# Products of the second block with one 512-column matmul over both parts of the activations, in units of two column tiles

## The chip, the cores and the metric

The kernel runs on one core of a Trainium2 chip. The metric is the device time of one execution in microseconds (us), taken as the median of several runs. Inside the core, TensorE (PE) multiplies matrices and accumulates into PSUM (8 banks of 512 fp32 values on each of 128 partitions); VectorE (DVE), ScalarE (ACT) and GpSimd (POOL) do elementwise work; SyncE (SP) issues the DMAs that bring the weights. "PEld" is TensorE's weight load, which runs beside its matmuls. A "column" of a matmul here is one token of the moving operand.

## The reference

Two blocks in sequence on 256 tokens of 2048 features. The first (a hybrid of a state-space part and a gated delta rule, with modulation) is not touched by the change. The second is two layers of differential attention with a gated short convolution beside it, and an MLP:

```python
def second_block(x, w_in, w_out, conv_w, q_norm_g, k_norm_g, ..., w_up, w_down, rel_bias):
    for l in range(DEPTH_2):                       # 2 layers
        h = _rmsnorm(x, attn_norm_g[l])
        proj = h @ w_in[l]                         # 2048 -> 6 * 1024
        q, k, v, gate_b, gate_c, conv_in = jnp.split(proj, splits, axis=-1)
        ...
        attn = _diff_attention(q, k, v, lam, rel_bias)      # 8 heads
        ...
        conv = gate_b * _short_conv(gate_c * conv_in, conv_w[l])
        x = x + jnp.concatenate([attn, conv], axis=-1) @ w_out[l]     # 2048 -> 2048
        hm = _rmsnorm(x, mlp_norm_g[l]) @ w_up[l]                     # 2048 -> 8192
        x = x + jnp.square(jax.nn.relu(hm)) @ w_down[l]               # 8192 -> 2048
    return x
```

All weights and activations are fp32.

## The kernel before

All big products work on numbers split in two: a high part, rounded to float32r, and a low part, the rest. A product of a weight W and an activation a is summed as hi(W)·hi(a) + hi(W)·lo(a) + lo(W)·hi(a).

Weights arrive in blocks of 512 KB (1024 columns of 128 partitions, `block`, L171). SP issues the load of a block (L177) into one of three `raw` buffers. Each block is split in two halves of 512 columns (`split`): ACT writes the high part (L143), and DVE the low part (L130), except that POOL writes the low parts of every fourth block. The high halves have four buffers and two more, the low halves four.

Activations are kept as pairs [128, 2, 4, 256]: part (high, low), K tile within a group of four, token. `pick` (L438) gives the two parts of one K tile.

`proj_steps` (L191) forms feature-major products: for each K tile of 128 features and each tile of 128 output columns, three matmuls of 256 columns, with the weights as the stationary operand. They all add into one accumulator `acc`, [128, 4, 256], which takes two banks of PSUM; there are two such accumulators (`pa`). A unit is four tiles of columns over all K tiles, 64 triples of matmuls for 16 K tiles, and a block of weights holds two K tiles of it. `proj_tok` (L224) does the values, with the activations as stationary operand and 512 columns of weights as the moving one.

`layer` (L1089) runs: the norm of the input (`norm_in`, L1038), which for the first layer makes its K tiles one after the other on DVE and ACT while the first products already use them; queries and keys (four units); values; then eight attention heads beside the gated convolution. The convolution has six units of eight blocks, 48 steps, and a head starts at each fifth step (`HEADS`, L1324). A head is a chain through the engines: scores on PE, scale and bias on DVE, exponentials on ACT, the difference of the two maps on DVE, transposes on PE (L150), a copy on ACT, the product with the values on PE. After it come `w_out` (four units), the norm, and the MLP, which alternates `up` (two units of 16 K tiles) and `down` (four units of eight K tiles, each added onto `x`). An accumulator is read by one DVE instruction of 1024 columns a unit, for example

```python
                ps = self.proj(wu, 4, act)
                t = self.t4(B)
                self.stt(t, ps, 0.0, rb, ALU.max, ALU.mult)
```

The order on each engine is made when the program is built, by a scheduler that simulates the engines; the generators `convs` and `heads` only give it the order of emission. In the rows below, lines L130, L133, L143, L146 and L150 are the helpers for DVE or POOL two-tensor operations, DVE three-operand ones, ACT, matmul and transpose.

Of the kernel before, what the change touches and what calls it, by code (L numbers as in the profile page):

```python
# [20 lines left out]
D = 2048  # L21
# [10 lines left out]
class Kern:  # L32
# [119 lines left out]
    def rsqrt(self, out, in_, mul, add, x, t):  # L152
        """out = 1/sqrt(in_*mul + add); x and t are scratch of the same shape."""
# [14 lines left out]
    def paced(self, out, in_):  # L168
        """A load that is not due yet, behind the last block of weights."""
# [3 lines left out]
    def block(self, ap, kt):  # L173
        """A block of weights in two parts, by K tile."""
# [16 lines left out]
    def proj_steps(self, w, nt, act, N=T, kts=range(NK), ps=None, fine=False):  # L191
        """Feature-major product: [128, nt, N] of nt tiles of columns over all K tiles, a block of weights a step
        or, if fine, a K tile."""
        ps = self.acc([128, nt, N]) if ps is None else ps
        per_bank = max(1, 512 // N)
        kts = list(kts)
        kt = CW // (nt * 128)
        for k0 in range(0, len(kts), kt):
            hv, lv = self.block(next(w), kt)
            for kk in range(kt):  # L200
# [15 lines left out]
            if not fine:  # L216
                yield ps

# [4 lines left out]

    def proj_tok(self, w, act):  # L224
        """Token-major product: [128, 2, 512] of four tiles of columns."""
        ps = self.acc([128, 2, 512])
        kt = CW // 512
        for k0 in range(0, NK, kt):
            hv, lv = self.block(next(w), kt)
            for kk in range(kt):  # L230
                k = k0 + kk
                (ah, al), = act(k)
# [8 lines left out]
    def sumsq_add(self, ps, src, first, last):  # L241
        """Add the squares of src [128, n, T], summed over features, to ps on every partition."""
# [88 lines left out]
    def ada_gate(self, m0):  # L331
        """Columns of four tiles from tile m0 for the tokens of x alone, as sums of scaled rows."""
# [25 lines left out]
    def side_step(self):  # L358
        """The part of the modulation that the end of the block needs goes along with its last products."""
# [7 lines left out]
    def block1_inputs(self, early, got):  # L367
        """The modulated inputs; early: the banks of projections that advance with them, four K tiles a step."""
# [33 lines left out]
        self.u_full = lambda k: self.pick(self.u[0])(k) + self.pick(self.u[1])(k)  # L402
# [35 lines left out]
    def pick(pairs):  # L438
        """K tile k of activations kept as pairs of parts, [128, 2, 4, T] for four tiles."""
# [1022 lines left out]
```

## Time and profile before

| | us |
|---|---|
| median of 3 runs | 3319.24 |
| lowest, highest | 3317.6, 3322.36 |
| profiled execution, span | 3319.0 |
| median less the span | 0.24 |
| first block (to the first product of the second) | 0 to about 1020 |
| second block, layer 0 | about 1020 to 2172 |
| of it: convolution and heads | 1206 to 1341 |
| of it: MLP | 1434 to 2172 |
| second block, layer 1 | about 2172 to 3314 |
| PE busy in the span | 3188.6 (96%) |
| DVE, ACT, POOL busy | 62%, 49%, 28% |
| granted TensorE clock, mean over the span | 0.988 |

PE is the engine that is nearly always busy. Since the ends of matmuls are modelled and overlap, the time that one really takes is read from the distance between the starts of consecutive ones, not from the durations. The profiled execution's own time is its span and the 0.24 us to the median of the runs.

### The profile page before, as it was taken

How to read it: one execution, taken by the hardware profiler on the slowest of the kernel's cores; microseconds unless marked ns; L12 is line 12 of the kernel's file. 1: busy time of each engine (PE TensorE's matmuls, PEld its weight loads, DVE VectorE, ACT ScalarE, POOL GpSimd, SP SyncE). 2: the span in 40 equal slices, each digit the busy share in tenths (PEclk: the TensorE clock that was granted, in tenths of full speed). 3: DMA queues.
4: the chain of work that ended last, by engine and by line, in shares of the span. 5: the costliest groups of instructions: out<-in, count | busy, mean ns of one | idle time of the engine just before them, and what ended most of it. 6: DMA issues, size and time to landing. Idle time of an engine off the chain costs nothing.

```text
span 3319.0 us, 65150 instructions
## 1 busy us (share of the span) xinstructions
PE 3188.6 (96%) x25258; PEld 3055.3 (92%) x25258; DVE 2072.2 (62%) x3665; ACT 1623.4 (49%) x3116; POOL 935.4 (28%) x739
## 2 busy tenths in 40 slices
PE   7899999998988999999999999999999999999999
PEld 3498888888887899999999999998999999999999
DVE  6878899998747567554444444555675544444444
ACT  6654444444544455454444444444554544444443
POOL 4614433233353222222222222222223222222221
PEclk9999999999999999999999999999999999999999
DMA  8733423334665455555555555555555555555555
GB/s 298 239 107 102 116 88 82 78 101 139 215 231 181 164 174 167 183 179 181 186 181 184 184 182 185 181 186 165 178 166 184 181 183 180 185 184 184 184 179 178
DMA packets 217607, 566.70 MB, mean 171 GB/s; under 512 B 45808, under 2 KB 69856, under 8 KB 217296
## 3 DMA queue, kind: packets, MB, share of 16 engines
q1 hardware_dynamic: 214976, 555.72, 52.0%
q0 software_dynamic: 1456, 4.65, 0.4%
q8 instruction: 198, 3.24, 0.4%
q10 hardware_dynamic: 864, 2.16, 0.2%
q14 instruction: 113, 0.93, 0.1%
HBM read 552.83 MB, written 9.63 MB: 169 GB/s over the span
## 4 chain that ended last, share of the span: by engine, by line
PE 75%; DVE 12%; DMA 5%; issue 2%; ACT 1%; POOL 1%; SPq 0%; DVEq 0%; ACTq 0%; POOLq 0%
PE acc L146 70%; DVE cc L133 2%; DVE lo L130 2%; PE ps L146 2%; PE p_pg L146 1%; PE p_pc L146 1%; DVE A L133 1%; DMA Am<-w_ada 1%; DVE b L130 1%; DMA W<-w_ada 1%; DMA g<-rows 1%; DMA A<-rows 1%; DVE g L133 1%; DMA raw<-w_in 1%; DVE x L133 0%
## 5 line engine op out<-in xcount | busy, mean ns | idle before, releaser
L146 PE MATMUL acc<-t,hi 128*128 128x256 f32 x12160 | 2228.7, 286 | 14.4 <-DVE t L133 6.3
L146 PEld LDWEIGHTS acc<-t,hi 128*128 128x128 f32 x12160 | 1888.6, 193 | 32.2 <-DVE t L133 9.3
L146 PE MATMUL acc<-t,lo 128*128 128x256 f32 x6080 | 1674.4, 286 | 16.5 <-DVE lo L130 15.5
L143 ACT ACTIVATE hi<-raw 128x512 fp32r<-128x512 f32 x1812 | 1092.9, 627 | 1220.6 <-PE acc L146 805.3
L130 DVE TENSOR_TENSOR lo<-raw,hi 128x512 fp32r<-128x512 f32 x1360 | 995.5, 736 | 803.5 <-PE acc L146 734.7
L146 PEld LDWEIGHTS acc<-t,lo 128*128 128x128 f32 x6080 | 1144.1, 193 | 24.0 <-DVE lo L130 20.0
L130 POOL TENSOR_TENSOR lo<-raw,hi 128x512 fp32r<-128x512 f32 x452 | 601.6, 1333 | 1873.3 <-PE acc L146 1440.3
L146 PE MATMUL acc<-c,hi 128*128 128x256 f32 x2560 | 463.9, 283 | 0.0
L146 PEld LDWEIGHTS acc<-c,hi 128*128 128x128 f32 x2560 | 399.4, 192 | 0.0
L146 PE MATMUL acc<-c,lo 128*128 128x256 f32 x1280 | 362.2, 283 | 0.0
L146 PEld LDWEIGHTS acc<-c,lo 128*128 128x128 f32 x1280 | 245.8, 192 | 0.0
L130 DVE TENSOR_TENSOR x<-x,acc 128x1024 f32<-128x1024 f32 x72 | 87.9, 1221 | 156.3 <-PE acc L146 156.3
L133 DVE SCALAR_TENSOR_TENSOR cc<-src,featv,cc 128x248 f32<-128x248 f32 (+2 forms) x224 | 132.7, 619 | 6.1 <-ACT cc L143 6.1
L133 DVE SCALAR_TENSOR_TENSOR t<-acc,t 128x1024 f32<-128x1024 f32 x32 | 39.2, 1225 | 68.2 <-PE acc L146 68.2
L146 PE MATMUL acc<-hi,t 128*128 128x512 f32 x256 | 81.2, 396 | 0.0
L143 ACT ACTIVATE t<-t 128x1024 f32<-128x1024 f32 (+1 forms) x56 | 59.4, 1060 | 26.5 <-DVE t L133 18.0
L130 POOL TENSOR_TENSOR Am<-A,masks 128x512 f32<-128x512 f32 x32 | 45.0, 1419 | 80.0 <-PE p_pg L146 26.8
L130 POOL TENSOR_TENSOR vT<-vT,W 128x512 f32<-128x512 f32 x28 | 41.3, 1474 | 74.8 <-ACT W L143 54.6
L146 PE MATMUL ps<-t,t 128*128 128x128 f32 (+2 forms) x320 | 60.9, 328 | 0.0
L146 PEld LDWEIGHTS acc<-hi,t 128*128 128x128 f32 x256 | 47.8, 188 | 10.5 <-issue 0.8
L146 PE MATMUL p_pg<-U,W 128*128 128x128 f32 (+1 forms) x384 | 47.0, 265 | 9.7 <-DVE W L130 9.5
L130 DVE TENSOR_TENSOR b<-b,b 64x1 f32<-64x1 f32 (+15 forms) x122 | 53.6, 439 | 2.1
(326 smaller groups left out, 2537.5 us busy)
## 6 DMA issues: line engine op xcount, KB each, us to landing
raw<-w_in SPq DMA_DIRECT2D x298, 512.0 KB, 3.7
raw<-w_up SPq DMA_DIRECT2D x256, 512.0 KB, 3.7
raw<-w_down SPq DMA_DIRECT2D x256, 512.0 KB, 3.9
raw<-w_out SPq DMA_DIRECT2D x96, 512.0 KB, 4.1
tok<-w_ada SPq DMA_DIRECT2D x77, 256.0 KB, 4.8
Am<-w_ada SPq DMA_DIRECT2D x57, 256.0 KB, 4.6
W<-w_ada SPq DMA_DIRECT2D x32, 256.0 KB, 4.2
kT<-w_ada SPq DMA_DIRECT2D x26, 256.0 KB, 4.3
```

The costliest lines, as they stand in the source:

```text
L130: return (eng or self.nc.vector).tensor_tensor(out=out, in0=in0, in1=in1, op=op)
L133: (eng or self.nc.vector).scalar_tensor_tensor(out=out, in0=in0, scalar=s, in1=in1, op0=op0, op1=op1)
L143: self.nc.scalar.activation(out=out, in_=in_, func=func, **kw)
L146: return self.nc.tensor.matmul(out, lhsT, rhs, start=start, stop=stop, skip_group_check=skip)
```

## The change

`product` replaces the three matmuls. For an accumulator with a fourth dimension, [128, 2, 2, 256] (tile, part, token), it does two: the high weights over both parts of the activations at once, 512 columns that fill a whole bank, read as two stretches of 256 columns that lie 1024 elements apart in the pair; and the low weights over the high part, 256 columns, onto the second half of the bank. The two halves are added when the accumulator is read: `sum2` copies one half on ACT and adds the other on DVE, `add2` adds both halves onto `x` with two DVE instructions. An accumulator still takes two banks, so that a unit is now two tiles of columns and a block of weights holds four K tiles of it. Queries, keys, convolutions, `w_out`, `up` and `down` use it; the values and the first block keep their matmuls. The weights are laid out on the host in the new order; the bytes loaded are the same. Comments and docstrings are taken out.

```diff
     def proj_steps(self, w, nt, act, N=T, kts=range(NK), ps=None, fine=False):
...
-        per_bank = max(1, 512 // N)
+        per_bank = 1 if isinstance(ps, list) or len(ps.shape) == 4 else max(1, 512 // N)
...
                     o = ps[n][:, 0] if isinstance(ps, list) else ps[:, n]
-                    outs = [o[:, s * T:s * T + T] for s in range(len(sides))]
-                    for s, (o, (ah, al)) in enumerate(zip(outs, sides)):
-                        st = i == 0 and s == 0 and n % per_bank == 0
-                        self.mm(o, hv[kk][:, c], ah, start=st, stop=False, skip=True)
-                        self.mm(o, hv[kk][:, c], al, start=False, stop=False, skip=True)
-                    for o, (ah, al) in zip(outs, sides):
-                        self.mm(o, lv[kk][:, c], ah, start=False, stop=last, skip=True)
+                    self.product(o, hv[kk][:, c], lv[kk][:, c], sides, i == 0 and n % per_bank == 0, last)
...
+    def product(self, o, hw, lw, sides, first, last):
+        if len(o.shape) == 3:
+            self.mm(o.rearrange("p a t -> p (a t)"), hw, sides, start=first, stop=False, skip=True)
+            self.mm(o[:, 1, :], lw, sides[:, 0, :], start=False, stop=last, skip=True)
+            return
...
+    def two_steps(self, w, act, kts=range(NK)):
+        return self.proj_steps(w, 2, act, kts=kts, ps=self.acc([128, 2, 2, T]))
...
+    def sum2(self, out, ps):
+        self.act(out, ps[:, :, 0, :])
+        self.tt(out, out, ps[:, :, 1, :], ALU.add)
+
+    def add2(self, x, ps):
+        for i in range(2):
+            self.tt(x, x, ps[:, :, i, :], ALU.add)
...
-        return lambda k: [(pairs[k // 4][:, 0, k % 4, :], pairs[k // 4][:, 1, k % 4, :])]
+        return lambda k: pairs[k // 4][:, :, k % 4, :]
...
         for u in range(4):
-            ps = self.proj(w, 4, act)
             t = self.t4(B)
-            self.tt(t, ps, rb)
+            for i in range(2):
+                self.sum2(t[:, 2 * i:2 * i + 2], self.two(w, act))
+            self.tt(t, t, rb)
...
         def convs():
-            for g in range(2):
-                for ps in self.proj_steps(w, 4, act):
+            for g in range(4):
...
+                for ps in self.two_steps(w, act):
                     yield
-                gc = self.t4(B)
-                self.tt(gc, ps, rb)
-                self.tt(gc, gc, rb)
+                self.sum2(gc, ps)
+                self.tt(gc, gc, r2)
+                self.tt(gc, gc, r2)
...
         for j in range(4):
-            ps = self.proj(w, 4, cact)
-            self.tt(self.x[j], self.x[j], ps, ALU.add)
+            for i in range(2):
+                self.add2(self.x[j][:, 2 * i:2 * i + 2], self.two(w, cact))
...
             for u in range(2):
-                ps = self.proj(wu, 4, act)
                 t = self.t4(B)
-                self.stt(t, ps, 0.0, rb, ALU.max, ALU.mult)
+                for i in range(2):
+                    self.sum2(t[:, 2 * i:2 * i + 2], self.two(wu, act))
+                self.stt(t, t, 0.0, rb, ALU.max, ALU.mult)
...
             for j in range(4):
-                ps = self.proj(wd, 4, hact, kts=range(8))
-                self.tt(self.x[j], self.x[j], ps, ALU.add)
+                for i in range(2):
+                    self.add2(self.x[j][:, 2 * i:2 * i + 2], self.two(wd, hact, kts=range(8)))
```

On PE at the start of the second block, before (`t_1808` holds the first four K tiles of the norm's output, `t_1809` the next four, `ps` the norm's sum of squares, `acc_12319` the first unit):

```order
L146 MATMUL acc_12319<-t_1808_12194,lo_1_12361 128x256
L146 MATMUL acc_12319<-t_1808_12194,hi_1_12360 128x256 x2
L146 MATMUL acc_12319<-t_1808_12194,lo_1_12361 128x256
L146 MATMUL acc_12319<-t_1809_12211,hi_0_12390 128x256
L146 MATMUL ps_12193<-t_1814_12266,consts 128x256
L146 MATMUL acc_12319<-t_1809_12211,hi_0_12390 128x256
L146 MATMUL acc_12319<-t_1809_12211,lo_0_12391 128x256
```

and the same place after the change, with a second unit, `acc_12427`:

```order
L146 MATMUL acc_12320<-t_1808_12194,hi_1_12327 128x512
L146 MATMUL acc_12320<-t_1808_12194,lo_1_12328 128x256
L146 MATMUL acc_12427<-t_1808_12194,hi_0_12430 128x512
L146 MATMUL acc_12320<-t_1808_12194,hi_1_12327 128x512
L146 MATMUL acc_12320<-t_1808_12194,lo_1_12328 128x256
L146 MATMUL acc_12320<-t_1808_12194,hi_1_12327 128x512
L146 MATMUL acc_12320<-t_1808_12194,lo_1_12328 128x256
L146 MATMUL ps_12193<-t_1814_12266,consts 128x256
L146 MATMUL acc_12320<-t_1809_12211,hi_0_12349 128x512
```

Each K tile now gives two products of the first unit instead of four, and products of the second unit stand among them. Ahead of the first product with K tile 15 stand 60 products before and 44 after.

On PE in the second half of the convolutions of layer 0, before (`ps_15493` takes a head's transposes, `acc_15720` a unit of a convolution):

```order
L146 MATMUL acc_15720<-t_1808_12194,hi_1_15727 128x256 x2
L146 MATMUL acc_15720<-t_1808_12194,lo_1_15728 128x256
L150 MATMUL ps_15493<-consts,t_2078_15510 128x128
L146 MATMUL acc_15720<-t_1808_12194,hi_1_15727 128x256 x2
L146 MATMUL acc_15720<-t_1808_12194,lo_1_15728 128x256
L146 MATMUL acc_15720<-t_1808_12194,hi_1_15727 128x256
L150 MATMUL ps_15493<-consts,t_2082_15524 128x128 x2
L146 MATMUL acc_15720<-t_1808_12194,hi_1_15727 128x256
L146 MATMUL acc_15720<-t_1808_12194,lo_1_15728 128x256
```

and after, for a head in the same half (`ps_14642` takes its transposes, `ps_14679` its product with the values, `ps_14825` and `ps_14826` are the scores of the next head, `acc_14742` the unit that ends and `acc_14905` the one that begins):

```order
L146 MATMUL acc_14742<-t_1811_12245,hi_1_14874 128x512
L146 MATMUL acc_14742<-t_1811_12245,lo_1_14875 128x256
L150 MATMUL ps_14642<-consts,t_2054_14659 128x128
L150 MATMUL ps_14642<-consts,t_2058_14673 128x128 x2
L146 MATMUL ps_14679<-t_1900_13270,t_2047_14641 128x128 x3
L146 MATMUL ps_14825<-t_1890_13232,t_1846_12541 128x128
L146 MATMUL ps_14825<-t_1890_13232,t_1846_12541 128x256
L146 MATMUL ps_14826<-t_1891_13233,t_1846_12541 128x128
L146 MATMUL ps_14826<-t_1891_13233,t_1846_12541 128x256
L146 MATMUL acc_14905<-t_1808_12194,hi_0_14908 128x512
```

The transposes stood amid a unit's products and now stand behind a unit's last product; the head's other matmuls, and the next head's scores, follow them ahead of the next unit.

On ACT at the same place, after the change (`t_2047` is the copy of the head's transposes, `acc_14586` the unit before `acc_14742`, whose accumulator `acc_14905` takes over):

```order
L143 ACTIVATE hi_0_14934<-raw_14932 128x512
L143 ACTIVATE hi_0_14960<-raw_14958 128x512
L143 ACTIVATE hi_1_14938<-raw_14932 128x512
L143 ACTIVATE hi_1_14964<-raw_14958 128x512
L143 ACTIVATE t_2047_14641<-ps_14642 128x384
L143 ACTIVATE t_2041_14584<-acc_14586 128x512
L143 ACTIVATE t_2021_14451,ssv_13634<-ps_14679 128x128 x2
```

The copy that reads the accumulator of the last unit but one stands behind the head's copy, which waits for the transposes.

## Rows read from the trace of the kernel before

**Rows 1.** The page: busy time of each engine, and the chain that ended last.

```profile
PE 3188.6 (96%) x25258; PEld 3055.3 (92%) x25258; DVE 2072.2 (62%) x3665; ACT 1623.4 (49%) x3116; POOL 935.4 (28%) x739
...
PE 75%; DVE 12%; DMA 5%; issue 2%; ACT 1%; POOL 1%; SPq 0%; DVEq 0%; ACTq 0%; POOLq 0%
PE acc L146 70%; DVE cc L133 2%; DVE lo L130 2%; PE ps L146 2%; PE p_pg L146 1%; PE p_pc L146 1%; DVE A L133 1%; DMA Am<-w_ada 1%; DVE b L130 1%; DMA W<-w_ada 1%; DMA g<-rows 1%; DMA A<-rows 1%; DVE g L133 1%; DMA raw<-w_in 1%; DVE x L133 0%
```

**Rows 2.** Busy time by stretch: us, busy (instructions) by engine, clock, DMA share, GB/s.

```profile
1020.00:1025.00 5.00, 4.73 (x27) 4.73 (x28) 3.90 (x14) 2.33 (x4) 0.00 (x0) 0.66 0.56 216
1035.00:1040.00 5.00, 3.50 (x18) 3.21 (x19) 5.00 (x7) 2.01 (x5) 3.19 (x3) 0.74 0.28 91
1020.00:1065.00 45.00, 40.65 (x293) 38.78 (x294) 38.90 (x75) 23.59 (x41) 17.41 (x16) 0.92 0.49 168
1206.00:1341.00 135.00, 133.11 (x1094) 131.67 (x1093) 99.96 (x199) 75.56 (x190) 30.41 (x28) 1.00 0.52 170
1434.00:2172.00 738.00, 738.00 (x6149) 737.92 (x6148) 365.53 (x477) 350.34 (x563) 175.21 (x136) 1.00 0.57 183
```

**Rows 3.** What PE waited for from 1020 on: us in total, times, longest.

```profile
PE acc L146 <- DVE t L133: 3.7, 6, 1.8
PE ps L150 <- DVE t L133: 3.0, 6, 0.9
PE ps L146 <- POOL t L130: 1.0, 1, 1.0
```

**Rows 4.** Groups of instructions from 1020 on: count, busy us, mean ns, idle before.

```profile
L146 PE MATMUL acc<-t,lo 128*128 128x256 f32 x4608 | 1306.7, 284 | 0.0
L143 ACT ACTIVATE hi<-raw 128x512 fp32r<-128x512 f32 x1530 | 920.7, 627 | 1091.4 <-PE acc L146 706.1 <-DMA raw<-w_in 115.1 <-DMA raw<-w_up 111.3
...
L130 DVE TENSOR_TENSOR lo<-raw,hi 128x512 fp32r<-128x512 f32 x1150 | 824.9, 720 | 768.7 <-PE acc L146 734.2 <-ACT hi L143 26.0 <-issue 6.0
L130 POOL TENSOR_TENSOR lo<-raw,hi 128x512 fp32r<-128x512 f32 x382 | 498.8, 1307 | 1680.9 <-PE acc L146 1435.3 <-ACT hi L143 182.5 <-DVE smx L1181 23.2
...
L146 PE MATMUL acc<-c,lo 128*128 128x256 f32 x1280 | 362.2, 283 | 0.0
```

**Rows 5.** PE's timeline in the MLP: start us, us, instruction.

```profile
1500.16 0.28 PE L146 MATMUL acc<-t,lo 128*128 128x256 f32 x1
1500.28 0.40 PE L146 MATMUL acc<-t,hi 128*128 128x256 f32 x2
1500.52 0.28 PE L146 MATMUL acc<-t,lo 128*128 128x256 f32 x1
```

**Rows 6.** PE's timeline in the values, 512 columns.

```profile
1130.11 0.39 PE L146 MATMUL acc<-lo,t 128*128 128x512 f32 x1
...
1133.51 0.39 PE L146 MATMUL acc<-lo,t 128*128 128x512 f32 x1
```

**Rows 7.** DVE's timeline as the first layer's norm begins and ends.

```profile
1019.74 0.48 DVE L133 SCALAR_TENSOR_TENSOR t<-x,featv,t 128x256 fp32r<-128x256 f32 x1
...
1050.45 0.47 DVE L133 SCALAR_TENSOR_TENSOR t<-x,featv,t 128x256 fp32r<-128x256 f32 x1
```

**Rows 8.** Tile hs: duration ns min/median/max, first and last start.

```profile
L130 DVE TENSOR_TENSOR hs<-hs,p_pc x8: 669/674/686, 274.9 to 377.0; 128x512 f32<-128x512 f32 x8
L143 ACT ACTIVATE hs<-acc x8: 572/580/598, 734.1 to 887.7; 128x512 f32<-128x512 f32 x8
```

**Rows 9.** Tile x, the same columns.

```profile
L130 DVE TENSOR_TENSOR x<-x,acc x72: 1220/1222/1223, 1363.8 to 3314.0; 128x1024 f32<-128x1024 f32 x72
...
L133 DVE SCALAR_TENSOR_TENSOR t<-x,featv,t x64: 469/478/1525, 1019.7 to 2578.7; 128x256 fp32r<-128x256 f32 x64
```

**Rows 10.** Timeline of a head: scores, transposes, the copy of them.

```profile
1277.74 2.03 PE L146 MATMUL ps<-t,t 128*128 128x128 f32 x13
...
1289.24 0.44 PE L150 MATMUL ps<-consts,t 128*128 128x128 f32 x2 [0.26 <-DVE t L133]
...
1289.71 0.49 ACT L143 ACTIVATE t<-ps 128x384 f32<-128x384 f32 x1
```

More of the change, by code (lines that the diff above doesn't have):

```diff
@@ L217, in proj_steps @@
                 yield ps
+    def product(self, o, hw, lw, sides, first, last):
[3 more added lines that the diff above has]
+            return
+        sides = sides if isinstance(sides, tuple) else (sides,)
+        outs = [o[:, s * T:s * T + T] for s in range(len(sides))]
+        for s, (q, p) in enumerate(zip(outs, sides)):
+            self.mm(q, hw, p[:, 0, :], start=first and s == 0, stop=False, skip=True)
+            self.mm(q, hw, p[:, 1, :], start=False, stop=False, skip=True)
+        for q, p in zip(outs, sides):
+            self.mm(q, lw, p[:, 0, :], start=False, stop=last, skip=True)
     def proj(self, *args, **kw):
@@ L222, in proj, with two @@
         return ps
+    def two_steps(self, w, act, kts=range(NK)):
+        return self.proj_steps(w, 2, act, kts=kts, ps=self.acc([128, 2, 2, T]))
+    def two(self, *args, **kw):
+        for ps in self.two_steps(*args, **kw):
+            pass
+        return ps
+    def sum2(self, out, ps):
[4 more added lines that the diff above has]
+            self.tt(x, x, ps[:, :, i, :], ALU.add)
     def proj_tok(self, w, act):
@@ L231, in proj_tok @@
                 k = k0 + kk
[L232 removed]
+                ah, al = act(k)[:, 0, :], act(k)[:, 1, :]
                 for c in range(2):
@@ L1215, in convs @@
         def convs():
-            for g in range(2):
-                for ps in self.proj_steps(w, 4, act):
+            cw = self.conv2.rearrange("p (l m k) -> p l m k", l=2, k=3)
+            B2 = [128, 2, 256]
+            r2 = r.unsqueeze(1).to_broadcast(B2)
+            for g in range(4):
+                if g % 2 == 0:
+                    cat[2 + g // 2] = pair = self.c8()
+                gc, p = self.t2(B2), self.t2(B2)
+                for ps in self.two_steps(w, act):
                     yield
-                gc = self.t4(B)
-                self.tt(gc, ps, rb)
-                self.tt(gc, gc, rb)
-                for ps in self.proj_steps(w, 4, act):
+                self.sum2(gc, ps)
+                self.tt(gc, gc, r2)
+                self.tt(gc, gc, r2)
+                for ps in self.two_steps(w, act):
                     yield
-                self.tt(gc, gc, ps)
-                cv = self.t4(B)
-                cw = self.conv2.rearrange("p (l m k) -> p l m k", l=2, k=3)
-                for i in range(4):
-                    wk = cw[:, l, 4 * g + i, :]
+                self.sum2(p, ps)
+                self.tt(gc, gc, p)
+                cv = self.t2(B2)
+                for i in range(2):
+                    wk = cw[:, l, 2 * g + i, :]
                     self.act(cv[:, i, :], gc[:, i, :], scale=wk[:, 2:3])
@@ L1232, in convs @@
                         self.stt(cv[:, i, o:256], gc[:, i, 0:256 - o], wk[:, k:k + 1], cv[:, i, o:256], ALU.mult, ALU.add)
-                self.tt(cv, cv, rb)
-                for ps in self.proj_steps(w, 4, act):
+                self.tt(cv, cv, r2)
+                for ps in self.two_steps(w, act):
                     yield
-                self.tt(cv, cv, ps)
-                pair = self.c8()
-                self.split(cv, pair[:, 0], pair[:, 1])
-                cat[2 + g] = pair
+                p = self.t2(B2)
+                self.sum2(p, ps)
+                self.tt(cv, cv, p)
+                h = slice(2 * (g % 2), 2 * (g % 2) + 2)
+                self.split(cv, pair[:, 0, h], pair[:, 1, h])
         hd, at = heads(), list(HEADS)
@@ L1275, in down @@
             for j in range(4):
-                ps = self.proj(wd, 4, hact, kts=range(8))
-                self.tt(self.x[j], self.x[j], ps, ALU.add)
+                for i in range(2):
+                    self.add2(self.x[j][:, 2 * i:2 * i + 2], self.two(wd, hact, kts=range(8)))
         up(0)
@@ L1411, in _pack @@
     p["w_out"] = _blocks(g["w_out"][0], [tiles(256 * j, 2) for j in range(8)])
[L1412 removed]
+    u2 = [tiles(256 * j, 2) for j in range(8)] + [tiles(512 * j, 4) for j in (4, 5)]
+    u2 += [tiles(o + 256 * j, 2) for j in range(4) for o in (4096, 5120, 3072)]
     p["w_in_2"] = np.stack([_blocks(w, u2) for w in g["w_in_2"]])
[L1414 to L1416 removed]
+    p["w_out_2"] = np.stack([_blocks(w, [tiles(256 * j, 2) for j in range(8)]) for w in g["w_out_2"]])
+    p["w_up_2"] = np.stack([_blocks(w, [tiles(256 * j, 2) for j in range(32)]) for w in g["w_up_2"]])
+    p["w_down_2"] = np.stack([np.concatenate([_blocks(w[1024 * s:1024 * s + 1024], [tiles(256 * j, 2) for j in range(8)])
                                               for s in range(8)]) for w in g["w_down_2"]])
```

6 lines of the change are left out of this document (1 added, 5 removed).

## Prediction

> **What bounds the kernel now.** I read the page first. It has PE busy 96% of the span, and the chain that ended last runs for 70% of the span through the products into `acc` [rows 1]: the kernel is bound by PE, and a change of its products counts in full wherever PE stays fed. Second, the stretches. In the MLP of layer 0 PE is busy for all of its 738 us at granted clock 1.00, the upper level (2.4 GHz), while DVE has 365.5 us and ACT 350.3. Among the convolutions and heads PE misses 135.00 - 133.11 = 1.9 us. At the start of the second block it misses 45.00 - 40.65 = 4.4 us, and the clock falls to 0.66 and 0.74 in two of its slices [rows 2]. Third, PE's waits from 1020 us on: together 7.7 us, all for the activations of the first norm or for a head, none for weights or for an accumulator [rows 3]. The waits of ACT and DVE are mostly for PE to give weight buffers back [rows 4], which says the same from their side.
>
> **A, the products.** The low-weight matmuls in the second block are 4608 + 1280 = 5888 [rows 4], one a triple, so there are 5888 triples (the values have another form and are not among them). A triple takes 1500.52 - 1500.16 = 0.36 us, 120 ns a matmul of 256 columns [rows 5]. For 512 columns there is a measurement in the values: five triples in 1133.51 - 1130.11 = 3.40 us, 226.7 ns a matmul [rows 6]. Doubling the columns thus adds 106.7 ns, and 13.3 ns of each matmul do not depend on them. A product becomes 226.7 + 120 = 346.7 ns instead of 360, if 512 columns in two stretches cost what 512 contiguous ones do. The sum is 5888 x 13.3 ns = 78.5 us off. No row shows a moving operand in two stretches. The nearest row is the contiguous one, and I take its price. The other end is that each stretch is paid like a matmul of its own, 240 ns, and nothing is saved. More than 78.5 us off is not seen either, since the columns stream at the same pace in both rows.
>
> The Trainium skill (page "TensorE: Matmul & The Clock Gate", section "Back-to-back issue gap") gives an isolated matmul a gap of N/2.4 + 2.5 ns. By it the three matmuls would take 327.5 ns and the two 325.0, and 2.5 ns x 5888 = 14.7 us would be saved instead of 78.5. The rows show 120 and 226.7 ns, not 109 and 216, and the measurement decides.
>
> **B, the start of the second block.** The 16 K tiles of the first norm come one by one, from 1019.74 to 1050.45 [rows 7], about 2.05 us apart. Before, each gives four products of the first unit (1.44 us). After, it gives two of the first unit, and what is run of the second unit follows in between. Ahead of K tile 15 the order has 44 products after the change and 60 before. When that tile arrives, 20 products stand to be done for the same 64 instead of 4: 16 x 0.347 = 5.5 us more. Against this, five DVE splits fewer stand ahead of that tile in the new order, 5 x 0.72 [rows 4] = 3.6 us earlier. That leaves about 2 us. PE also idles more on the way, in a stretch where its clock was granted at 0.66 and 0.74 in two slices [rows 2]; I add 2 us for that, half of what PE misses there now, and take +4. The ends are 0 (the earlier K tile covers all) and +9 (the 5.5 us, and 3.5 for waits and the lower clock).
>
> **C, the convolutions and heads.** Each head's transposes stood amid a unit; they now stand behind a unit's last product, at five boundaries a layer (heads 3 to 7). The next unit takes the accumulator of the last but one, whose copy on ACT stands behind the copy of the head's transposes. From the last transpose on there follow one after the other the head's copy, 0.49 us [rows 10], the accumulator's copy on ACT, 0.58, and the addition on DVE, 0.674 [rows 8], with some 0.3 for the handovers (a PE wait of 0.26 us in the row of the transposes is of this size [rows 10]): 2.1 us. Beside them PE has the product with the values (three matmuls of 128 columns) and the next head's scores, four of 128 or 256 columns, 7 x 0.156 = 1.1 us by the row of 13 such matmuls in 2.03 us [rows 10]. So PE idles about 1.0 us at four boundaries and 0.65 at the other, 5 us a layer, +10 for two. The lower end is 0. For the upper end take a head's chain that is late itself: in the new order a head's scores stand at one boundary and its transposes at the next, four blocks of 2.77 us or 11.1 us later. From the end of the scores (1277.74 + 2.03) to the transposes (1289.24) it takes 9.5 us now [rows 10], which leaves 1.6 us of play. If the chain gets half as long again on the fuller DVE and ACT, PE waits some 3 us more at eight boundaries: 34.
>
> **D, the accumulators' readers.** Instead of one DVE instruction of 1024 columns (1.222 us) `x` gets two of 512 (2 x 0.674 = 1.35). At the very end that is +0.1 us. Elsewhere they lie beside PE. In a layer's MLP there are 32 units of `up`, each with 0.58 more on ACT and 0.674 on DVE, and 64 of `down`, each with 1.35 - 0.61 = 0.74 more on DVE: DVE gets 21.6 + 47.4 = 69 us, ACT 18.6. The MLP takes 738 - 2048 x 0.0133 = 711 us, and DVE is then busy for 365.5 + 69 = 434 (61%), ACT 369 (52%). A unit of `down` lasts 16 x 0.347 = 5.5 us and its accumulator is read in 1.35, so that PE is free to run on in the other one. If this cover went, all of it on PE's path would cost 2 x 69 = 138 us.
>
> **E, the weights.** The bytes are the same in less time: 183 GB/s x 738 / 711 = 190, at a DMA share of 0.57 x 1.04 = 0.59 [rows 2]. The waits of PE name no weights now [rows 3]; nothing is added. POOL's share of the splits (382 of 1307 ns [rows 4]) is unchanged. A block lasts 8 x 0.347 = 2.77 us, four of them 11.1, and POOL needs 2.6 of these.
>
> **Sum.** -78.5 + 4 + 10 + 0.1 = -64.4 us. 3319.0 (span) + 0.24 (to the median) - 64.4 = 3254.8; I say 3255.
>
> **Rivals.**
> - *The ends of units and the start cost nothing* (B and C zero): 3319.2 - 78.4 = 3241. For it: the waits for heads are only 3 us now [rows 3], and a scheduler's order can be early as well as late. Against it: the order on ACT, with the accumulator's copy behind the head's.
> - *Heads are late at the new boundaries*, C at its upper end with +3 us at eight boundaries: 3255 + 24 = 3279. For it: 9.5 of the 11.1 us between boundaries are used already. Against it: the chain waits partly behind weight splits whose order changed too, and those can be shorter.
> - *The second stretch costs a fixed share of its own* (slower): A is 0, the rest stays: 3319.2 + 14.1 = 3333. This is a mechanism on PE's read of the moving operand; it outweighs the gain when the second stretch costs more than (78.5 - 14.1) / 5888 = 10.9 of the 13.3 ns. For it: no row shows such an operand. Against it: nothing in the trace charges for the way an operand lies.
> - *DVE falls behind beside POOL.* The row `t<-x,featv` has a median of 478 ns and a longest of 1525 [rows 9], so that a DVE instruction on SBUF can be stretched by 1.05 us. In a unit of `down`, DVE has 3 splits of 0.72 and the two additions, 3.5 of 5.5 us; two stretched splits of three would reach the bound, and three would make it 6.66, 1.1 us too long. Over 128 units that is +141, 3396. Against it: the mean of the splits is 0.72 over 1150 of them [rows 4], so hardly any is stretched now. The page "SBUF — State Buffer" of the Trainium skill (section "Who interferes with whom") says that DVE and GpSimd share a pair of ports under an exclusive lock; the stretched row agrees, and the mean shows how rarely it bites.
> - *Little of the fixed share goes*: at 14.1 / 5888 = 2.4 ns a product the gain and the new waits cancel, 3319. For it: the split into 106.7 and 13.3 ns comes from two places with different operands. Against it: both rows are of the same engine at the same clock. The page's rule on the gap between matmuls, above, is of this kind.
>
> **How the numbers follow.** Forecast 3255: 0.50, its own range 3246 to 3266 (B from 0 to 9, C from 5 to 16). No cost at B and C, 3241: 0.22. Late heads, 3279: 0.13. Second stretch paid in full, 3333: 0.07, of which 0.01 lands within the bound. Little of the share, 3319: 0.03. DVE behind, 3396 or a part of it: 0.05, half of it still faster. What a measurement tells from no change here is about 0.2%, 6.6 us. Faster: 0.50 + 0.22 + 0.13 + 0.025 = 0.875, say 0.88; same 0.04; slower 0.08. The range for 8 in 10 reaches from below the case without costs, 3236, to the far side of late heads, 3288.
>
> **What would show it.** In the profile after, PE's starts in the MLP should lie 0.347 us apart a product, with clock 1.00 and 711 us for layer 0's MLP (A). If they are 0.36 apart, A is wrong. From 1020 to 1065, PE's idle time should grow by a few us (B). In the convolutions, waits of PE for DVE's addition into `t` should show about 1 us each at some ten places (C); waits of 3 us for the transposes would mean the second rival. PE should have no waits for weights and DVE about 61% in the MLP (D, E). The prediction fails if PE's starts are uneven there, with DVE, ACT or a load ahead of them.

## The result, and the profile after

The changed kernel takes 3280.56 us (median of 4 runs, 3271.82 to 3284.87) against 3320.78 before: 40 us less, ratio 0.9875 with a 95% interval of [0.9858, 0.9893]. Forecast were 3255 and 64 us less. The way was right, 24 us of the size were not there.

The page after, busy time by engine, for [rows 1]:

```profile
PE 3121.5 (95%) x19370; PEld 2736.6 (84%) x19370; DVE 2190.9 (67%) x4009; ACT 1669.7 (51%) x3224; POOL 934.5 (29%) x739
```

The stretches that answer to [rows 2] (the first begins where the second block does, 1022 us in this trace):

```profile
1022.00:1069.00 47.00, 36.34 (x168) 27.52 (x167) 41.60 (x79) 24.13 (x42) 15.46 (x15) 0.89 0.48 156
1206.00:1341.00 135.00, 128.49 (x752) 111.70 (x751) 98.42 (x219) 80.83 (x205) 28.92 (x26) 1.00 0.52 165
1434.00:2133.00 699.00, 699.00 (x4033) 616.32 (x4032) 398.31 (x586) 353.97 (x581) 169.18 (x131) 1.00 0.60 190
2600.00:3200.00 600.00, 600.00 (x3463) 529.07 (x3462) 338.36 (x488) 302.64 (x493) 142.05 (x109) 1.00 0.60 190
```

In the MLP PE is still busy throughout, now with two matmuls a product: 699 / (4033 / 2) = 346.6 ns, where [rows 2] has 738 / (6149 / 3) = 360.1. PE misses 10.7 of the first 47 us of the second block. Before, counted from the end of the first block too, it missed 5.8:

```profile
1017.60:1064.60 47.00, 41.22 (x293) 38.57 (x292) 40.81 (x80) 25.05 (x44) 17.01 (x16) 0.93 0.52 179
```

Among the heads it misses 6.5 us instead of 1.9. PE's waits from 1030 us on, for [rows 3]:

```profile
PE ps L146 <- ACT t L143: 11.1, 10, 1.7
PE acc L146 <- DVE t L133: 5.1, 6, 1.7
PE acc L146 <- ACT hi L143: 2.0, 1, 2.0
PE acc L146 <- DVE t L130: 1.3, 4, 0.4
PE acc L146 <- POOL lo L130: 1.3, 1, 1.3
```

New is the first row: ten waits of a head's matmul for ACT's copy of the transposes. New too are two waits for weights, one for a high part from ACT and one for a low part from POOL. PE's timeline in the MLP, for [rows 5]:

```profile
1500.06 0.28 PE L146 MATMUL acc<-t,lo 128*128 128x256 f32 x1
1500.17 0.39 PE L146 MATMUL acc<-t,hi 128*128 128x512 f32 x1
1500.40 0.28 PE L146 MATMUL acc<-t,lo 128*128 128x256 f32 x1
1500.52 0.39 PE L146 MATMUL acc<-t,hi 128*128 128x512 f32 x1
```

A long matmul steps 230 ns and a short one 117: together 347, as forecast.

The second block by stages, in us, each from the start of one matmul to that of another in the timeline (the last matmul of the first block, the first of the values of layer 0, the last transposes of its heads, the first of the values of layer 1, the last transposes there, the last product). "A" is the number of products of the stage times 13.3 ns, "lost" the rest, against the mean of the two traces before:

| stage | before (2 traces) | after | A | lost |
|---|---|---|---|---|
| start, queries and keys | 111.4, 109.7 | 115.5 | -3.4 | 8.4 |
| values, heads, convolutions | 204.0, 204.4 | 205.2 | -5.1 | 6.1 |
| w_out, MLP, queries and keys of layer 1 | 938.7, 938.7 | 907.8 | -34.1 | 3.2 |
| values, heads, convolutions | 203.4, 203.7 | 204.6 | -5.1 | 6.2 |
| w_out, MLP | 838.6, 838.6 | 809.3 | -30.7 | 1.4 |
| all | 2296.1, 2295.1 | 2242.5 | -78.5 | 25.3 |

So the profiled run gains 53 us in the second block. It is the fastest of the four; the others are 5 to 13 us longer, and the experiments had to find that too.

### The profile page after: what moved, and what is told of

The parts are those of the page before. It is cut to its first block, busy times and chain, and to the rows that moved or that the text cites. A ratio compares the mean times of both kernels' runs of the same rounds, so it can differ in the third digit from the quotient of the medians.

```text
span 3270.1 us, 53719 instructions
## 1 busy us (share of the span) xinstructions
PE 3121.5 (95%) x19370; PEld 2736.6 (84%) x19370; DVE 2190.9 (67%) x4009; ACT 1669.7 (51%) x3224; POOL 934.5 (29%) x739
## 4 chain that ended last, share of the span: by engine, by line
PE 73%; DVE 12%; DMA 6%; issue 3%; ACT 2%; POOL 1%; SPq 0%; DVEq 0%; ACTq 0%; POOLq 0%
PE acc L146 68%; DVE lo L130 2%; DVE cc L133 2%; PE ps L146 2%; DMA Am<-w_ada 1%; DMA raw<-w_in 1%; PE p_pg L146 1%; DVE b L130 1%; PE p_pc L146 1%; DVE A L133 1%; DMA g<-rows 1%; DVE t L133 1%; DMA A<-rows 1%; DMA W<-w_ada 1%; ACT hi L143 1%
## 5 line engine op out<-in xcount | busy, mean ns | idle before, releaser
L146 PE MATMUL acc<-t,hi 128*128 128x512 f32 (+1 forms) x7552 | 2173.6, 355 | 18.3 <-DVE t L133 9.9
L146 PEld LDWEIGHTS acc<-t,hi 128*128 128x128 f32 x7552 | 1312.6, 191 | 229.1 <-DVE t L133 12.9
L130 DVE TENSOR_TENSOR lo<-raw,hi 128x512 fp32r<-128x512 f32 x1360 | 979.1, 728 | 371.0 <-PE acc L146 282.3
L146 PE MATMUL acc<-c,hi 128*128 128x512 f32 x1280 | 450.4, 391 | 0.0
L130 DVE TENSOR_TENSOR x<-x,acc 128x512 f32<-128x512 f32 x288 | 197.6, 686 | 179.5 <-PE acc L146 176.5
L130 DVE TENSOR_TENSOR t<-t,acc 128x512 f32<-128x512 f32 x104 | 71.3, 687 | 337.4 <-ACT t L143 337.4
L146 PEld LDWEIGHTS acc<-c,hi 128*128 128x128 f32 x1280 | 239.4, 187 | 52.9
L146 PE MATMUL ps<-t,t 128*128 128x128 f32 (+2 forms) x320 | 61.9, 331 | 11.1 <-ACT t L143 11.1
L146 PEld LDWEIGHTS ps<-t,t 128*128 128x128 f32 (+1 forms) x320 | 42.6, 174 | 23.9 <-ACT t L143 13.6
L133 DVE SCALAR_TENSOR_TENSOR t<-t,t 128x1024 f32<-128x1024 f32 (+2 forms) x68 | 59.9, 882 | 0.6
L143 ACT ACTIVATE t<-acc 128x512 f32<-128x512 f32 x104 | 60.1, 580 | 0.0
```

The source lines that it names most:

```text
L130: return (eng or self.nc.vector).tensor_tensor(out=out, in0=in0, in1=in1, op=op)
L133: (eng or self.nc.vector).scalar_tensor_tensor(out=out, in0=in0, scalar=s, in1=in1, op0=op0, op1=op1)
L143: self.nc.scalar.activation(out=out, in_=in_, func=func, **kw)
L146: return self.nc.tensor.matmul(out, lhsT, rhs, start=start, stop=stop, skip_group_check=skip)
```

## The experiments

Second blocks below are "all" of the table, read in the same way; times of one group of runs are compared with the kernel before on the same chip.

**The changed kernel again.** No edit.

> The changed kernel once more, unchanged. The four runs so far lie between 3271.8 and 3284.9, the profiled one at the fast end. Theory S (the spread is jitter of the first block, whose instructions are the same, since the two profiles at hand differ by 4.5 us at its end): a profile of another run is longer by what the first product of the second block is later, and from there to the end it takes the same as in the profile after within 2 us. Rival: the spread comes from the second block, where waits of PE for ACT or for weights change from run to run; then the stretch from the first product to the end differs by several us. Time expected: 3272 to 3285, median about 3280.

Measured: 3287.64 us (3285.13 to 3294.11), ratio 0.9898 [0.9885, 0.9911]. The first block ended at 1021.4 us, 0.7 earlier than in the trace after, so theory S fails. The second block took 2256.4, 13.9 more, and all of it (824.2 against 809.3) in the last stage. PE's timeline there, in the MLP of layer 1:

```profile
2590.47 0.28 PE L146 MATMUL acc<-t,lo 128*128 128x256 f32 x1
2590.59 0.39 PE L146 MATMUL acc<-t,hi 128*128 128x512 f32 x1
2590.82 0.28 PE L146 MATMUL acc<-t,lo 128*128 128x256 f32 x1
...
2591.33 0.49 PE L146 MATMUL acc<-t,hi 128*128 128x512 f32 x1
2592.68 0.39 PE L146 MATMUL acc<-t,lo 128*128 128x256 f32 x1 [0.85 <-POOL lo L130]
...
2593.25 0.40 PE L146 MATMUL acc<-t,hi 128*128 128x512 f32 x1
2593.49 0.28 PE L146 MATMUL acc<-t,lo 128*128 128x256 f32 x1
2593.61 0.40 PE L146 MATMUL acc<-t,hi 128*128 128x512 f32 x1
2593.84 0.28 PE L146 MATMUL acc<-t,lo 128*128 128x256 f32 x1
2593.96 0.40 PE L146 MATMUL acc<-t,hi 128*128 128x512 f32 x1
```

and its stretches:

```profile
1434.00:2100.00 666.00, 666.00 (x3844) 582.78 (x3844) 375.24 (x549) 334.04 (x547) 159.26 (x122) 1.00 0.61 191
2600.00:3200.00 600.00, 600.00 (x3399) 520.73 (x3398) 329.91 (x477) 299.45 (x486) 139.19 (x108) 1.00 0.60 186
```

Up to 2591 the long matmuls step 230 ns. There PE waits once, 0.85 us, for a low part from POOL. After it three products in turn step 241 + 120, 236 + 113 and 233 + 117 ns, and so to the end: 600 / (3399 / 2) = 353.0 ns a product, against 600 / (3463 / 2) = 346.5 after (353.3 and 346.7 by the distances between starts). PE is busy throughout in both, waits for nothing that the profile shows, and the clock is granted at 1.00 in both. So neither supply nor clock shows as a cause: it is a second steady rhythm of the same two matmuls, 6.6 ns a product slower; 2048 products in it are 13.5 us. Neither trace of the kernel before has one: there all steps of the MLP are 120 ns.

**Three matmuls in the new units.**

```diff
-            self.mm(o.rearrange("p a t -> p (a t)"), hw, sides, start=first, ...)
+            self.mm(o[:, 0, :], hw, sides[:, 0, :], start=first, ...)
+            self.mm(o[:, 1, :], hw, sides[:, 1, :], start=False, ...)
```

> The changed kernel with its units of two tiles, its readers and its layout, but each product again as three matmuls of 256 columns: high weights times high part into the first half of the bank, high times low and low times high into the second. Theory (the 512-column matmul alone brings the gain, 13 ns a product, 5888 products): 76.5 us slower than the changed kernel, 3350 to 3360, and slower than before by the losses at the start and among the heads, some 25 to 35 us; PE's starts in the MLP 120 ns apart. Rival (part of the gain comes from the smaller units or their readers): 3300 to 3330, with less than 50 us lost.

Measured: 3344.42 us (3339.49 to 3345.9), ratio 1.0063 [1.005, 1.0076]: 57 to 64 us slower than the changed kernel. By the traces the second block is 2313.1, 70.6 longer than after; its MLP stages of 941.3 and 841.2 us are 33.5 and 31.9 longer, where 13.3 ns would make it 34.1 and 30.7. There the 512-column matmul alone brings the gain. Among the heads it brings little: their two stages take 205.9 and 205.5 us, only 0.7 and 0.9 more than after, where 768 products at 13.3 ns make 10.2. Without the long matmul units and readers cost 17 us against before (2313.1 - 2295.6), half of them at the start. The comparison of medians comes out smaller, as it would if the changed kernel had the slow rhythm in some of its runs.

**The first unit of layer 0 as before.**

```diff
+            if u == 0 and l == 0:
+                self.tt(t, self.proj(w, 4, act), rb)
+            else: ...
```

> The changed kernel, but the first unit of layer 0 (queries, four tiles) again as one unit of four tiles with three matmuls, as before the change; all else as after. Theory B (the start costs about 9 us, since each K tile of the norm feeds only two products and the first matmul needs both parts): some 8 us faster than the changed kernel (9 back, 64 x 13 ns = 0.8 lost), about 3272, with PE missing 10 to 11 us between 1010 and 1060 instead of 17 to 20. Rival (what PE lacks there is the norm's own pace, the same for any order): no difference, 3280.

Measured: 3287.76 us in two clusters, 3279.6 to 3282.7 and 3292.8 to 3299.7; ratio 0.9899 [0.9879, 0.9919]. No gain. PE's waits from 1030 us on:

```profile
PE ps L146 <- ACT t L143: 13.7, 10, 2.3
PE acc L146 <- DVE t L130: 6.3, 5, 5.0
```

In the first 40 us of the second block PE lost 11.5 us beyond steps of 120 and 227 ns, 4 less than after (15.9), but at 1068 us it waited 5.0 us for DVE to read the old unit's accumulator, an addition that stood behind the chain of the norm's root on DVE. The cost had moved. This trace has the slow rhythm too, in the MLP of layer 1 after three waits for POOL (2.2 us in all): its last stage takes 825.8 us. The means of the two clusters lie 16 us apart, about what the rhythm costs in one MLP.

**Heads at every sixth step.**

```diff
-HEADS = range(0, 40, 5)
+HEADS = range(2, 48, 6)
```

> The changed kernel, but the heads start at steps 2, 8, ..., 44 of the 48 instead of 0, 5, ..., 35. In the order most of their transposes then stand amid a unit, with 22 to 27 matmuls between them and the product with the values; two a layer instead of four have only the unit's end. Theory C (PE waits 1.1 to 1.7 us for ACT's copy of the transposes where the product with the values stands right behind them): PE's waits for the copy fall from 11.1 us to 5 or less, and the time by 6 to 10 us, to about 3272. Rival (the wait moves: the last heads are later, and w_out or the next unit waits for them): waits for the copy fall, others rise as much, and the time stays within 3 us of the changed kernel's.

Measured: 3298.6 us (3295.96 to 3306.85), ratio 0.9934 [0.9922, 0.9946], 11 us slower than the changed kernel on the same chip. PE's waits from 1030 us on:

```profile
PE acc L146 <- DVE t L133: 10.5, 9, 2.2
PE ps L150 <- DVE t L130: 6.7, 2, 3.8
...
PE ps L146 <- ACT t L143: 3.6, 4, 1.9
```

The waits for the copy fell as expected, 11.1 to 3.6 us, and the rival came true with more than its price: the last head starts at step 44, its chain ends after the convolutions, and PE loses some 12 and 14 us in front of the two `w_out`.

**The two parts of a K tile side by side.**

```diff
-        return self.t8([128, 2, 4, T], FR)
+        return self.t8([128, 4, 2, T], FR).rearrange("p k a t -> p a k t")
```

> The changed kernel, but in the second block the two parts of a K tile lie beside each other in the pair, so that the 512 columns are one contiguous stretch. In the traces so far PE keeps one of two rhythms in the MLP: 230 + 117 ns a product (sum 346.7), or, in two profiles from a stall of 1.1 us in layer 1 on, 232 to 241 + 113 to 120 (sum 353.3). Theory R (the slow rhythm comes from the jump between two stretches): steps of 227 + 120 ns and no slow rhythm in any profile, runs within 6 us of each other, median about 3272. Rival P (it comes from the alternation of a long and a short matmul with their weight loads, whatever the operand's place): the same spread and median as the changed kernel, 3281 to 3288, and the slow rhythm can be found again.

Measured: 3271.3 us, runs of 3268.79, 3269.81, 3272.79 and 3282.76; ratio 0.9856 [0.9837, 0.9874]. PE's timeline in the MLP:

```profile
1500.18 0.28 PE L146 MATMUL acc<-t,lo 128*128 128x256 f32 x1
1500.30 0.39 PE L146 MATMUL acc<-t,hi 128*128 128x512 f32 x1
1500.53 0.28 PE L146 MATMUL acc<-t,lo 128*128 128x256 f32 x1
1500.65 0.39 PE L146 MATMUL acc<-t,hi 128*128 128x512 f32 x1
```

The steps are 230 and 117 ns as with two stretches: a jump of 1024 elements costs nothing, and theory R's 227 + 120 is wrong. The profiled run kept the fast rhythm, even across a wait like the one at which it was lost above:

```profile
2590.26 0.39 PE L146 MATMUL acc<-t,lo 128*128 128x256 f32 x1 [0.85 <-POOL lo L130]
2590.49 0.39 PE L146 MATMUL acc<-t,hi 128*128 128x512 f32 x1
2590.72 0.28 PE L146 MATMUL acc<-t,lo 128*128 128x256 f32 x1
2590.84 0.40 PE L146 MATMUL acc<-t,hi 128*128 128x512 f32 x1
```

So such a wait does not always bring the slow rhythm. Whether parts side by side keep it away stays open: one trace can't tell, and that one of four runs is 13 us longer speaks for the rival, but no trace of that run shows its rhythm.

**New products in w_out and the MLP only.** Queries, keys and `convs()` with their layout from before.

> The new products and units only in w_out and the MLP (4608 of the 5888 products); queries, keys and convolutions as before the change, so that the start of the second block and the heads have their old order. Theory BC (the start costs 9 us and the heads 16): -61 us from products and nothing lost, 3321 - 61 = 3260, plus up to 27 where the slow rhythm holds in both MLPs; about 8 us faster than the changed kernel. PE's waits from 1030 us on about 8 us, none for ACT's copy. Rival (the losses at the start and the heads come with any new order, or are jitter of the first block): about 16 us slower than the changed kernel, 3297.

Measured: 3256.52 us (3254.49 to 3263.21), ratio 0.9808 [0.9793, 0.9823]: 4608 products gain 64 us where 5888 gained 40. PE's waits from 1030 us on:

```profile
PE ps L150 <- DVE t L133: 3.0, 5, 0.9
PE acc L146 <- DVE t L133: 2.7, 3, 1.8
```

These two rows lead [rows 3] too, none is for ACT's copy, and theory BC's 3260 is met within 4 us. The second block takes 2235.6 us, 7 less than after, with the old start (111.2) and shorter stages of heads (202.9, 204.2). Between the two profiled runs another 6.6 us are the earlier end of the first block (1015.5 against 1022.1). For the rest of the 24 us between the medians there is no trace; runs in the slow rhythm could be a reason.

**No low parts from POOL in the second block.**

```diff
             self.scope2(s)
+            self.share = 0
```

> The changed kernel, but in the second block DVE writes all low parts and POOL none. The slow rhythm began in two profiles at a stall of PE for a low part that POOL had written, 1.1 us after the start of layer 1's MLP. Theory G (a late low part from POOL throws PE into the slow rhythm): no waits for POOL, no slow rhythm, runs close together at about 3272; DVE about 80% busy in the MLP. Rival (any stall can set the rhythm, or DVE is now late itself): PE waits for DVE's low parts, 3285 or more, above all among the convolutions, where DVE had 99 of 135 us.

Measured: 3274.65 us (3269.02 to 3275.49), ratio 0.9853 [0.9837, 0.987]. Stretches of its MLPs:

```profile
1434.00:1800.00 366.00, 365.98 (x2109) 320.17 (x2108) 245.48 (x367) 184.92 (x306) 2.37 (x2) 1.00 0.59 190
1850.00:2050.00 200.00, 199.43 (x1136) 173.27 (x1135) 129.41 (x193) 97.32 (x161) 0.00 (x0) 1.00 0.58 185
2800.00:3200.00 400.00, 400.00 (x2306) 349.55 (x2305) 269.23 (x397) 200.04 (x327) 0.00 (x0) 1.00 0.59 189
```

347.1, 352.1 and 346.9 ns a product: the slow rhythm holds from 1894 to 1957, where it begins with a wait of 0.6 us for DVE, from 1985 to 2047, from 2637 to 2719 and from 2745 to 2809, where it begins without a wait in the profile. It went again all four times, each time at a place where the order has two long matmuls one right behind the other, as the third row here:

```profile
1957.19 0.40 PE L146 MATMUL acc<-t,hi 128*128 128x512 f32 x1
1957.42 0.28 PE L146 MATMUL acc<-t,lo 128*128 128x256 f32 x1
1957.54 0.64 PE L146 MATMUL acc<-t,hi 128*128 128x512 f32 x2
1958.02 0.28 PE L146 MATMUL acc<-t,lo 128*128 128x256 f32 x1
1958.13 0.39 PE L146 MATMUL acc<-t,hi 128*128 128x512 f32 x1
```

Before it a product steps 353 ns, after it 347. Theory G fails: the slow rhythm needs no late part from POOL. The waits for DVE's low parts are 1.1 us in all, with DVE 67% busy, so the rival's 3285 fails too.

**The kernel before again.** No edit.

> The kernel before, unchanged, for a second trace. In the first trace the first matmul of the second block began at 1018.8 us, in the four of changed kernels with the same first block 2 to 9 us later. Theory J (jitter of the first block's loads and waits): this trace differs from the first by 2 us or more there too. Rival (the new kernels slow the first block in some way): 1019 again, within 1 us. PE's steps in the MLP 120 ns throughout, without a second rhythm.

Measured: 3323.52 us (one run). The last matmul of its first block starts at 1021.3 us, 3.7 later than in the first trace; in all traces it lies between 1015.5 and 1027.3. Theory J holds: the first block varies by itself, and its end is no effect of the change.

**Convolutions as before, the rest new.** `convs()` and its layout from before.

> The changed kernel, but the convolutions as before the change (units of four tiles, three matmuls), so that the heads stand amid units again; queries, keys, w_out and MLP stay new. Theory C (the heads' waits and the drained PE around them cost about 8 us a layer): 768 products lose 10 us and 16 come back, some 6 us faster than the changed kernel, 3275 to 3280 beside its 3281 to 3288; PE's waits for ACT's copy are gone. Rival (the start alone makes the version with only w_out and the MLP so fast): about 8 us slower than the changed kernel, 3290 or more.

Measured: 3263.74 us (3257.6 to 3269.08), ratio 0.9818 [0.9803, 0.9834]. No wait for ACT's copy is left. By the medians, of two chips, that is 17 us better than the changed kernel, but by the traces in the same rhythm only 2 (2240.8 against 2242.5): of the 12.3 us lost around the heads the old units give back little more than the 10.2 that their products lose. The trace is of the slowest run, though. The other three are 5 to 11 us faster, by something that no trace shows. Theory C's direction and the end of the waits are shown, its 6 us are not.

**Queries and keys as before, the rest new.**

> The changed kernel, but queries and keys of both layers as before the change; convolutions, w_out and MLP stay new. Theory B (the start costs 9 us): 512 products lose 6.8 us and 9 come back, 0 to 4 us faster than the changed kernel; PE misses 10 to 13 us between 1000 and 1100 us beyond its steps instead of 19 to 21. Rival (as with the first unit alone: the wait moves to the accumulator at the change from old to new units): a stall of several us at the first new unit, and no gain or a loss.

Measured: 3265.35 us (3263.79 to 3267.22), ratio 0.9824 [0.9811, 0.9837]. The start stage takes 110.5 us instead of 115.5, although 256 products of it lost their 3.4, and no stall stands at the change of units: theory B holds, and the loss at the start was 8 us. The second block is 2237.9, 4.6 less than after, and the two profiled runs differ by as much (3267.22 against 3271.82). The medians lie 15 us apart; no trace shows where the rest comes from.

**Both long matmuls first, then both short ones**, on the version with `w_out` and MLP only.

```diff
+                    for n, c in enumerate(cs):
+                        self.mm(ps[:, n].rearrange("p a t -> p (a t)"), hv[kk][:, c], sides, ...)
+                    for n, c in enumerate(cs):
+                        self.mm(ps[:, n, 1, :], lv[kk][:, c], sides[:, 0, :], ...)
```

> The version with the new products in w_out and the MLP only, but for each K tile the two matmuls of 512 columns first and then the two of 256. Theory (a slow rhythm needs a long and a short matmul in turn): no slow rhythm; 347 ns a product or less, all runs within 5 us, 3250 to 3258. Rival (the step of a matmul does not depend on its neighbours): the same 3256 with the same spread of 9 us. If two short matmuls one after the other cost 120 each and two long ones 227, nothing changes in the sum.

Measured: 3269.96 us (3265.05 to 3271.68), ratio 0.9835 [0.9822, 0.9849]; 2241.9 for the second block, 6.3 more than with the matmuls in turn. A stretch of its MLP:

```profile
2600.00:3200.00 600.00, 600.00 (x3447) 523.54 (x3446) 334.90 (x485) 304.59 (x489) 139.83 (x108) 1.00 0.59 189
```

600 / (3447 / 2) = 348.1 ns a product, 1.6 more, which for 4608 products is 7.4 us. The step does depend on the neighbours, and this order is a third rhythm. Both expectations fail, though the trace has no slow rhythm. (Between the two profiled runs another 6.6 us are the later end of the first block, 1022.1 against 1015.5.)

**Queries and keys of layer 1 new as well**, on the same version.

> The version with the new products in w_out and the MLP, and in the queries and keys of layer 1 too, where the norm's K tiles do not come one by one while the products start. Theory (only the first layer's start loses): 256 x 13.3 ns = 3.4 us less, 3253. Rival (two readers a unit instead of one, or the short end of a unit before the next, cost as much): 3256 or more.

Measured: 3260.24 us (3258.03 to 3261.47), ratio 0.9808 [0.9795, 0.9821], the same ratio as without. By the traces the second block is 2.1 us shorter (2233.5), all of it in the stage that holds layer 1's queries and keys (906.5 against 908.7). That is 1.2 short of the theory's 3.4, the medians, of two chips, go the other way, and two traces of the kernel before differ by 1.0: undecided.

The lowest median is that of the version with new products in `w_out` and the MLP, 3256.5 us.

## Why the prediction was right, and where not

- **A, the products**: right in mechanism and price where PE is the bound. In the MLP 346.6 ns were measured for 346.7, two stretches cost nothing, and three matmuls in the same units lose the gain again. By the Trainium skill's rule of 2.5 ns for an isolated matmul (page "TensorE: Matmul & The Clock Gate", section "Back-to-back issue gap") the estimate was 14.7 us; the measurement decides for 13.3 ns. Two things failed. The sum counts the gain in full among the heads as well, but there the joined matmul brought 1.6 of 10.2 us. And the price was taken as one number: PE can settle at 353.3, which costs 14 us an MLP layer. No row of the trace before shows it, and no rival had it. The two clusters of the run with the first unit as before lie 16 us apart, which agrees, and it may be why the median lies 9 us above the profiled run. But the end of the first block varies by up to 12 us between the traces of all versions, and the other three runs have no trace, so this is not shown.
- **B, the start**: right in kind, sized at 4, measured 8.4, within its bounds (0 to 9). K tile 15 came only some 2.5 us earlier than before, not 3.6, and 26 of 64 products had not started when it came, not 20. The first matmul now needs both parts: PE waited 2.2 us for DVE's low part there (first row below), where before it waited 1.1 us for ACT's high part (last row). And the two new waits for weights stand in this stretch (second and third row); the sum had nothing for them.

```profile
1024.86 0.47 PE L146 MATMUL acc<-t,hi 128*128 128x512 f32 x1 [2.17 <-DVE t L133]
1030.69 0.80 PE L146 MATMUL acc<-t,hi 128*128 128x512 f32 x1 [2.02 <-ACT hi L143]
1056.63 0.39 PE L146 MATMUL acc<-t,lo 128*128 128x256 f32 x1 [1.27 <-POOL lo L130]
```

```profile
1019.27 0.38 PE L146 MATMUL acc<-t,hi 128*128 128x256 f32 x1 [1.08 <-ACT t L143]
```

- **No term**: the two stages with `w_out` and the MLP lost 3.2 and 1.4 us. With layer 1's queries and keys as before, the first of them loses 2.1, so that some 1.1 of its 3.2 belong to that start.
- **C, the heads**: sized at 10, measured 12.3. The place was right, the order of the waits was not. PE does not run the product with the values beside the copies: that product needs the head's copy itself, and the copy stood behind two weight splits on ACT. The rows after, on PE and then ACT, at one such boundary:

```profile
1280.20 0.44 PE L150 MATMUL ps<-consts,t 128*128 128x128 f32 x2 [0.28 <-DVE t L133]
1281.89 2.25 PE L146 MATMUL ps<-t,t 128*128 128x128 f32 x14 [1.26 <-ACT t L143]
```

```profile
1280.31 1.15 ACT L143 ACTIVATE hi<-raw 128x512 fp32r<-128x512 f32 x2 [1.08 <-DMA raw<-w_in]
1281.37 0.47 ACT L143 ACTIVATE t<-ps 128x384 f32<-128x384 f32 x1
1281.74 0.59 ACT L143 ACTIVATE t<-acc 128x512 f32<-128x512 f32 x1
```

The first row of ACT holds the two splits, the second the head's copy. The splits had themselves waited 1.08 us for their weights' load. At all ten boundaries two or three splits stand right ahead of the copy, and the first of them waited 0.2 to 2.1 us for a load. By the time that the scores are done the accumulator is nearly free (1.3 us of waits for DVE in all), so that the price came out alike by another path: that was luck. By the run with three matmuls in the same units only 3.7 of the 12.3 us come from units and readers; the other 8.6 are the part of A that was not gained here.

- **D and E**: right in their rates. DVE is 57% busy in the MLP (61 forecast), ACT 51% (52), and the weights come at 190 GB/s at a share of 0.60 (190, 0.59). But E added nothing for waits, and there are the 3.3 us of B's two rows and the loads behind the heads' copies.
- **The base**: the profiled runs take 1.7 to 2.0 us beyond their span, not the 0.24 that the median of three runs suggested; before is 3320.8.

The sum: -78.5 + 25.3 = -53 in place of -64.4. Of the 24 us that were missing, 11 are B, C and the stages without a term, mis-sized or left out. The other 13 lie outside the second block of the profiled run: some 4 are the later end of its first block, and 9 lie between it and the median. They were not in the list of causes.

The measured 3280.6 lies outside the forecast's own 3246 to 3266 and beside the 3279 of the rival with late heads. That is chance too: the rival had 34 us at the heads, which cost 12.3.

What makes PE settle in one rhythm or the other stays open. Shown is that it changes at short waits in some places and at none in others, that the fast one can outlast the same wait, that the slow one goes on for 600 us with the clock granted at 1.00 and no wait in the profile, that side-by-side parts do not alter the fast one, and that the order of long and short matmuls matters: two long and two short ones in turn take 348.1 ns, and the four times that PE came back to the fast rhythm two long ones stood in a row.

## What to carry to other kernels

A matmul's fixed share, read from two lengths in the same trace, predicts well what joining matmuls saves where PE is the bound. Where it isn't, at starts that feed PE tile by tile and at chains through several engines, smaller units take the gain back. A short copy that such a chain needs can stand on its engine behind work that waits for a load. So a change of this kind is worth making stage by stage. When runs of a new kernel spread wider than those of the old one, compare the steps of single instructions between two traces before looking for a stall.

## What was not expected of the hardware

The same two matmuls, 512 and 256 columns with full supply and the clock granted at 1.00, run in steady rhythms of 346.7 or 353.3 ns a product in one program. They pass from the fast one to the slow one at a wait of under 1 us, or at none that shows, and were seen to pass back only where two long ones stood in a row. With two long and two short ones in turn the product takes 348.1.
